# Two buffers for a state space's scratch tile and rotation tables, and another PSUM bank for its last products

## The chip, the cores and the metric

The kernel runs on one core of one Trainium2 chip. The metric is device time in microseconds (us) of one execution: the median of several runs. The core has a matrix engine (TensorE, PE in the profile, with PEld for its weight loads), a vector engine (VectorE, DVE), a scalar engine (ScalarE, ACT), GpSimd (POOL) and a queue engine (SyncE, SP) that issues most of the transfers. Each runs its own instructions in a fixed order, and they wait for one another by semaphores.

## What is computed

One inference step of one hybrid decoder layer (width 1024) for a new prompt of 512 positions and for eight running sequences that get one token each. Cut to what matters here:

```python
def hybrid_layer(x, c, ssm_s0, attend, lp):
    mod = jnp.dot(jax.nn.silu(c), lp['w_ada']) + lp['b_ada']
    sh1, sc1, gt1, sh2, sc2, gt2 = jnp.split(mod, 6, axis=-1)
    proj = jnp.dot(modulate(x, lp['norm_attn'], sh1, sc1), lp['w_in'])
    u, q, k_c, v_c, k_s, v_s, k_w, v_w, g = jnp.split(proj, offsets, axis=-1)
    o_ssm, s_last = ssm_mixer(u, ssm_s0, lp)             # complex diagonal state space, 32 groups
    o_attn, win_state = attend(q, gates, kv_cmp, kv_slc, kv_win)   # sparse attention
    mix = jnp.concatenate([rmsnorm(o_ssm, ...), rmsnorm(o_attn, ...)], axis=-1)
    x = x + gt1[:, None, :] * jnp.dot(mix, lp['w_out'])
    h2 = modulate(x, lp['norm_mlp'], sh2, sc2)
    x = x + gt2 * jnp.dot(jnp.square(jax.nn.relu(jnp.dot(h2, lp['w_up']))), lp['w_down'])

def ssm_mixer(u, s0, lp):                # per group: s_t = lam * s_(t-1) + B u_t ;  y_t = Re(C s_t) + d u_t
    ...
    z = jax.nn.gelu(y)
    return z * jax.nn.sigmoid(jnp.dot(z, lp['ssm_w_glu'])), s_last
```

## The kernel before, in words

Activations lie transposed in SBUF, features on the 128 partitions and the 520 positions (512 and 8) along the free side. Large products take every operand as a high and a low part (`split`: ACT casts the high part, DVE subtracts for the low part, L63 and L64) and issue three matmuls for each pair of tiles. PSUM has eight banks. In the first part of the kernel they are shared out by tag: `pj` 2, `ss` 2, `tr` 2, `ad` 1, `po` 1; `pst(tag, name)` takes the next bank of a tag and so waits until its last user has been read.

The stages follow each other roughly like this: preparation and the projection of `u` (L605 with tile `pj`, to 120 us); the compression of cached keys and values (`compressed`, L382 to L402: transposes `pxc` L368, evictions `xc` on ACT and DVE, products `ph` L387, then `pk` L396 and L398 in the bank `po`); the state space, which runs among it; the projections of keys and values (`kv_proj(0..2)`, loads `wkv` L627, products `pkv` L647) and of the conditioning (`ada`, loads `wada` L330, products `pada` L334); the projection of q (`proj_half`, L605 again, evictions `ql` and `QS` L912 to L914); attention of the prompt (scores `pst` L1217 to L1219, maxima `mxa` L1223, exponentials `pe` L1227, scaling L1232, transposes `ptp` L1246, evictions `PT` L1249, products `po` L1253) woven with that of the eight sequences (`pkT` L1023, `ktS` L1026 and L1028, `pS` L1032, `tS` L1034 and L1010, `smx` L1009, `ppt` L1049, `ptS` L1050, `ppn` L1052); the output projection (`pwo`); and from 525 us the MLP (`pup`, `pdn`, L1401).

Ahead of the state space the values `u` are written to DRAM through the scratch tile `ut` (tag `tmp`, L616) and read back regrouped as `U` (L722 to L725). The state space itself takes the 32 groups in eight **quads** of four groups. A quad makes, on DVE, the tables `BP` and `Cb` through `tmp` (L752 to L759); on PE the products `pm` and transposes `pbb` (L766, L767), evicted as `M0` and `Bb`; from `M0`, through DRAM, the Toeplitz matrix `Tz` (L772, L774); the rotation tables `CT` and `ST` (L776 to L781, from `cmul`, L486 to L488); then `pvs` = Bb x U (L792), evicted as `Vs`, turned by CT and ST into `W`, scanned along time (`Rr`, L803), turned back into `Sx` (L808 to L815); and last the products `pys` (L819: U with Tz, L820: Sx with Cb, eight matmuls in turn), evicted as `ys` (L821) and written to DRAM (L822). After the last quad the final states go through `psf` (L827) and the tile `so` (L828) out to DRAM. `state_space_outputs` (L884 and on) reads the results back one quarter at a time as `yc` (L888), one buffer, and makes `yf` (L890, L893) and the GELU `zt` (L108 to L113); one quarter follows each of `kv_proj(1)`, `kv_proj(2)` and the two halves of the projection of q.

In SBUF most tiles of the state space have one buffer each; `ss`, with two banks, serves `pm0`, `pbb`, `pvs`, `pys` and `psf` of the state space and, later, parts of attention (`psc`, `pS`, `poS`).

The order of instructions on each engine is not that of the code. The program is laid out by a scheduler that simulates a timeline: an instruction is placed when its operands and its buffer are free by the simulated times. So a buffer more or less can change what stands where on all five engines.

Of the kernel before, what the change touches and what calls it, by code (L numbers as in the profile page):

```python
# [9 lines left out]
F32 = mybir.dt.float32  # L10
# [6 lines left out]
P = 128  # L17
D = 1024
T = 512
# [17 lines left out]
def body(tc, i, o, dbg=None):  # L37
# [19 lines left out]
    def pst(tag, name):  # L57
        return bank["tile"].tile([P, 512], F32, tag=tag, name=name, bufs=bank["tags"][tag])
# [9 lines left out]
    def rawt(name):  # L68
        return raw.tile([P, 2048], F32, tag="raw", name=name)
# [101 lines left out]
    def wsplit(r, more=0):  # L171

        if more:
            h, l = (bank["wq"].tile([P, KT, P], F32R, tag="wq" + c, name="wq" + c, bufs=2) for c in "HL")
        else:
            h, l = whl(*r.shape[1:])
        split(h, l, r)
        return h, l
# [34 lines left out]
    GQ = 4  # L213
# [222 lines left out]
    ss = p0.tile([P, 5], F32, name="ss")  # L436
# [48 lines left out]
    def cmul(outr, outi, ar_, ai_, br_, bi_, tmp):  # L485
        nc.vector.tensor_tensor(outr, ar_, br_, ALU.mult)  # L486
        nc.vector.tensor_tensor(tmp, ai_, bi_, ALU.mult)
        nc.vector.tensor_tensor(outr, outr, tmp, ALU.subtract)  # L488
        nc.vector.tensor_tensor(outi, ar_, bi_, ALU.mult)
        nc.vector.tensor_tensor(tmp, ai_, br_, ALU.mult)  # L490
        nc.vector.tensor_tensor(outi, outi, tmp, ALU.add)
# [102 lines left out]
    sl = slx.enter_context(tc.tile_pool(name="sl", bufs=1, reuse_waits="tile"))  # L594
# [3 lines left out]
    def proj_half(wh, wl):  # L598

        for hf in range(2):  # L600
            ps = pst("pj", "pj")
            hc = slice(hf * HB, (hf + 1) * HB)
            for k in range(KT):
                for n, (w, x) in enumerate(((wh, hH), (wh, hL), (wl, hH))):
                    nc.tensor.matmul(ps[:, 0:HB], w[:, k], x[:, k, hc], start=(k == 0 and n == 0), stop=(k == KT - 1 and n == 2))  # L605
            yield hf, ps[:, 0:HB]

    for s in range(2):
        r = rawt("wu").rearrange("p (k c) -> p k c", k=KT)
        nc.sync.dma_start(r, i["w_in"][0, :, s * 256 : (s + 1) * 256].rearrange("(k p) c -> p k c", p=P))  # L610
        for m in range(2):
            wh, wl = wsplit(r[:, :, m * P : (m + 1) * P])
            q = 2 * s + m
            for hf, ps in proj_half(wh, wl):
                nc.scalar.copy(uT[:, q, hf * HB : (hf + 1) * HB], ps)
            ut = sl.tile([P, T], F32, tag="tmp", name="ut")  # L616
            nc.vector.tensor_copy(ut.rearrange("p (t c) -> p c t", t=8), uT[:, q, 0:T].rearrange("p (c t) -> p c t", t=8))
            nc.sync.dma_start(uscr[q * P : (q + 1) * P, 0:T], ut)
            nc.sync.dma_start(uscr[q * P : (q + 1) * P, T:NT], uT[:, q, T:NT])
# [107 lines left out]
    for qd in range(NG // GQ):  # L727
# [14 lines left out]
        b4 = [P, GQ, 8, 16]  # L742
# [4 lines left out]
        def vec_b(x):  # L747
            return x.unsqueeze(2).to_broadcast(b4)

        tmp = sl.tile(b4, F32, tag="tmp", name="tmp")  # L750
        BP = sl.tile(b4, F32, tag="BP", name="BP")
        nc.vector.tensor_tensor(BP, lam_b(lr, 0), vec_b(P1[:, gs]), ALU.mult)  # L752
        nc.vector.tensor_tensor(tmp, lam_b(li, 0), vec_b(P1p[:, gs]), ALU.mult)
        nc.vector.tensor_tensor(BP, BP, tmp, ALU.subtract)
        tmp = sl.tile(b4, F32, tag="tmp", name="tmp")
        Cb = sl.tile(b4, F32, tag="Cb", name="Cb")
        nc.vector.tensor_tensor(Cb, lam_b(lr, 1), vec_b(C1[:, gs]), ALU.mult)
        nc.vector.tensor_tensor(tmp, lam_b(li, 1), vec_b(C1p[:, gs]), ALU.mult)
# [14 lines left out]
        mw = mscr[qd, 0:P]  # L773
        nc.sync.dma_start(Tz, bass.AP(tensor=mw.tensor, offset=mw.offset, ap=[[GQ * 16, P], [16 * GQ * 16, 8], [1, GQ * 16]]))  # L774

        CT = sl.tile([P, GQ, 8, 8], F32, tag="CT", name="CT")  # L776
        ST = sl.tile([P, GQ, 8, 8], F32, tag="ST", name="ST")
        tq = sl.tile([P, GQ, 8, 8], F32, tag="tq", name="tq")
        b8 = [P, GQ, 8, 8]
        ab = [tab[:, x, 1, gs].unsqueeze(3).to_broadcast(b8) for x in range(2)] + [tab[:, x, 0, gs].unsqueeze(2).to_broadcast(b8) for x in range(2)]  # L780
        cmul(CT, ST, *ab, tq)  # L781
        CT = CT.rearrange("p g a b -> p g (a b)")
        ST = ST.rearrange("p g a b -> p g (a b)")
        rho = sl.tile([P, GQ, 64], F32, tag="rho", name="rho")
# [13 lines left out]
        W2 = sl.tile([P, GQ, 64], F32, tag="W2", name="W2")  # L798
        nc.vector.tensor_tensor(W, Vs[:, :, 0:64], CT, ALU.mult)
        nc.vector.tensor_tensor(W2, Vp, ST, ALU.mult)  # L800
        nc.vector.tensor_tensor(W, W, W2, ALU.add)
# [6 lines left out]
        nc.gpsimd.memset(Sx[:, :, 0:1], 0.0)  # L808
        nc.vector.tensor_tensor(W2, Rp, ST, ALU.mult)
        nc.vector.tensor_tensor(W, Rr, CT, ALU.mult)  # L810
        nc.vector.tensor_tensor(Sx[:, :, 1:65], W, W2, ALU.subtract)
# [1 line left out]
        nc.gpsimd.memset(Sx[:, :, 64:72], 0.0)  # L813
        nc.vector.tensor_copy(Sx[:, :, 72:80], s0[:, :, gs].rearrange("p b g -> p g b"))
        ys = sl.tile([P, GQ, 80], F32, tag="ys", name="ys")  # L815
        py = pst("ss", "pys")
        for g in range(GQ):
            c = slice(g * 80, (g + 1) * 80)
            nc.tensor.matmul(py[:, c], Tz[:, :, :, g].rearrange("p t c -> p (t c)"), U[:, qd * GQ + g], start=True, stop=False)  # L819
# [5 lines left out]
    for n in range(2):  # L825
        nc.tensor.transpose(px[:, n * P : (n + 1) * P], sn[:, 4 * n : 4 * n + 4].rearrange("p b g -> p (b g)"), ident)
    nc.tensor.transpose(px[0:NG, 256:384], SF, ident)  # L827
    so = sl.tile([P, 384], F32, name="so")  # L828
    nc.vector.tensor_copy(so[:, 0:256], px[:, 0:256])
    nc.vector.tensor_copy(so[0:NG, 256:384], px[0:NG, 256:384])  # L830
    for n, nm in enumerate(("re", "im")):
# [485 lines left out]
    for n in range(16):  # L1317
        j, br, hh = n // 4, n // 2 % 2, n % 2
        if n % 4 == 0:
            po = pst("po", "po")  # L1320
# [275 lines left out]
```

## Time and profile before

| | |
|---|---|
| median of 3 runs | 896.05 us (895.32 to 898.2) |
| the profiled execution | 896.29 us, its span 894.6 us |
| granted clock over the span (share of full) | 0.992 |
| PE busy | 844.3 us, 94% |
| DVE busy | 525.0 us, 59% |
| ACT busy | 388.2 us, 43% |
| POOL busy | 65.2 us, 7% |
| state space: first `pvs`, last `pys` | 138.5 us, 258.4 us |
| projection of q, attention, output projection, MLP begin | 267, 297, 451, 525 us |

The span is the profiled part of the execution; the time of the execution is 1.69 us longer. An engine is busy while at least one of its instructions is executing, so a stretch minus PE's busy time in it is the time in which PE did nothing.

### The profile page before, as it was taken

The numbers are of one execution on the slowest core, as the hardware profiler recorded it, in microseconds if no ns is written. First come the engines' busy times: TensorE is split into PE (matmuls) and PEld (weight loads), VectorE is DVE, ScalarE is ACT, GpSimd is POOL, SyncE is SP. The second block draws the span as 40 slices with busy tenths as digits, with TensorE's granted clock in tenths as the row PEclk, the third lists the DMA queues.
The fourth block names the chain that finished last, engine by engine and source line by source line (L and its number), as shares of the span: only waits on it lengthen the run. The fifth ranks groups of instructions, "written<-read, shape, count | busy, mean of one in ns | idle before, by whom it ended". The sixth has DMA issues, their size and how long they took to land.

```text
span 894.6 us, 16415 instructions
## 1 busy us (share of the span) xinstructions
PE 844.3 (94%) x6517; PEld 747.3 (84%) x6517; DVE 525.0 (59%) x1413; ACT 388.2 (43%) x880; POOL 65.2 (7%) x147
## 2 busy tenths in 40 slices
PE   3799998999999899999889999999999999999995
PEld 2567897788998676756579999999999999999995
DVE  6676656759747975667578964443233444434534
ACT  2545326634435656546655554441111344433422
POOL 6001201000134200100000000000000000000000
PEclk9999999999999999999999999999999999999998
DMA  8956678366456620303257552333333333332202
GB/s 294 318 193 217 194 169 239 123 204 194 127 179 206 203 95 1 142 1 142 78 206 227 161 189 85 95 95 95 95 95 95 95 95 95 96 88 70 79 1 95
DMA packets 111836, 122.36 MB, mean 137 GB/s; under 512 B 24500, under 2 KB 91880, under 8 KB 109584
## 3 DMA queue, kind: packets, MB, share of 16 engines
q1 hardware_dynamic: 102256, 89.71, 33.0%
q0 software_dynamic: 5488, 29.99, 9.8%
q10 hardware_dynamic: 4016, 1.62, 0.7%
q8 instruction: 51, 0.84, 0.4%
q14 instruction: 25, 0.20, 0.1%
HBM read 112.47 MB, written 13.03 MB: 140 GB/s over the span
## 4 chain that ended last, share of the span: by engine, by line
PE 86%; DMA 6%; ACT 3%; DVE 2%; issue 1%; SPq 0%; ACTq 0%; DVEq 0%
PE pdn L1401 21%; PE pup L1401 20%; PE pj L605 5%; PE pwo L1401 5%; PE pkv L647 5%; PE ph L387 5%; DMA wada<-w_ada 5%; PE pada L334 2%; PE ptp L1246 2%; PE po L1253 2%; PE pS L1032 2%; PE pg L1273 2%; PE pst L1217 2%; PE pys L819 2%; PE pkT L1023 1%; PE pst L1218 1%
## 5 line engine op out<-in xcount | busy, mean ns | idle before, releaser
L1401 PE MATMUL pdn<-hidL,wH 128*128 128x256 f32 (+1 forms) x480 | 136.1, 284 | 0.0
L1401 PE MATMUL pdn<-hidH,wL 128*128 128x256 f32 (+1 forms) x480 | 135.9, 283 | 0.0
L1401 PE MATMUL pdn<-hidH,wH 128*128 128x256 f32 (+1 forms) x480 | 135.4, 282 | 0.0
L1401 PE MATMUL pup<-h2L,wH 128*128 128x256 f32 (+1 forms) x480 | 135.0, 282 | 0.0
L1401 PE MATMUL pup<-h2H,wL 128*128 128x256 f32 (+1 forms) x480 | 135.0, 282 | 0.0
L1401 PE MATMUL pup<-h2H,wH 128*128 128x256 f32 (+1 forms) x480 | 134.1, 283 | 0.0
L1401 PEld LDWEIGHTS pup<-h2L,wH 128*128 128x128 f32 x480 | 90.4, 188 | 0.8 <-DVE rs_t L97 0.8
L1401 PEld LDWEIGHTS pdn<-hidH,wL 128*128 128x128 f32 x480 | 90.6, 189 | 0.0
L1401 PEld LDWEIGHTS pdn<-hidL,wH 128*128 128x128 f32 x480 | 90.4, 188 | 0.1
L1401 PEld LDWEIGHTS pup<-h2H,wL 128*128 128x128 f32 x480 | 90.4, 188 | 0.0
L1401 PEld LDWEIGHTS pdn<-hidH,wH 128*128 128x128 f32 x480 | 90.4, 188 | 0.0
L1401 PEld LDWEIGHTS pup<-h2H,wH 128*128 128x128 f32 x480 | 89.6, 188 | 0.0
L63 ACT CAST wH<-wdn 128x1024 fp32r<-128x1024 f32 x30 | 31.5, 1050 | 114.0 <-PE pdn L1401 104.1
L64 DVE TENSOR_TENSOR wL<-wup,wH 128x1024 fp32r<-128x1024 f32 x30 | 36.7, 1224 | 58.1 <-ACT wH L63 58.1
L64 DVE TENSOR_TENSOR wL<-wdn,wH 128x1024 fp32r<-128x1024 f32 x30 | 36.8, 1225 | 54.2 <-ACT wH L63 54.2
L387 PE MATMUL ph<-xc,w 128*128 128x256 f32 (+2 forms) x320 | 65.4, 356 | 1.2 <-DVE xc L377 0.7
L387 PEld LDWEIGHTS ph<-xc,w 128*128 128x128 f32 x320 | 52.8, 203 | 12.9 <-issue 6.4
L63 ACT CAST wH<-wup 128x1024 fp32r<-128x1024 f32 x30 | 31.5, 1050 | 48.0 <-PE pup L1401 37.6
L1479 ACT ACTIVATE rl<-pup 128x256 f32<-128x256 f32 (+1 forms) x64 | 24.4, 384 | 48.9 <-PE pup L1401 48.8
L375 ACT COPY xc<-pxc 64x256 f32<-64x256 f32 x96 | 32.1, 366 | 20.8 <-DVE xc L377 18.2
L1410 DVE SCALAR_TENSOR_TENSOR xT<-pdn,mod,xT 128x256 f32<-128x256 f32 x32 | 15.2, 479 | 43.2 <-PE pdn L1401 43.2
L1480 DVE TENSOR_TENSOR rl<-rl 128x256 f32<-128x256 f32 (+1 forms) x64 | 27.1, 425 | 22.6 <-ACT rl L1479 22.6
(557 smaller groups left out, 2023.9 us busy)
## 6 DMA issues: line engine op xcount, KB each, us to landing
wada<-w_ada SPq DMA_DIRECT2D x20, 1024.0 KB
wup<-w_up SPq DMA_DIRECT2D x16, 1024.0 KB
wdn<-w_down SPq DMA_DIRECT2D x16, 1024.0 KB
wo<-w_out SPq DMA_DIRECT2D x8, 1024.0 KB
wada<-w_ada SPq DMA_DIRECT2D x8, 512.0 KB
rwin<-state_win SPq DMA_DIRECT2D x4, 1024.0 KB
new_win_sample<-state_win POOLq DMA_DIRECT2D x2, 2044.0 KB, 8.9
wkv<-w_in SPq DMA_DIRECT2D x3, 1024.0 KB
```

What stands on the lines that cost most here:

```text
L63: nc.scalar.copy(h, src)
L64: nc.vector.tensor_tensor(l, src, h, ALU.subtract)
L334: nc.tensor.matmul(ps[k % 4 * 32 : k % 4 * 32 + 32], cT[:, k], rs[k // kp][:, k % kp], start=(k < 4), stop=(k >= 4))
L375: nc.scalar.copy(dst[:, :, :, hf], srcv[:, :, :, hf])
L387: nc.tensor.matmul(phv[:, lo:hi, 0:w], w1[n][:, r_], xc[n][:, lo:hi, r_ % 8, off : off + w], start=(r_ == 0), stop=(r_ == 15))
L605: nc.tensor.matmul(ps[:, 0:HB], w[:, k], x[:, k, hc], start=(k == 0 and n == 0), stop=(k == KT - 1 and n == 2))
L647: nc.tensor.matmul(ps[0:mp, 0:nw], x[:, k, tok], w[:, k % 4], start=(k == 0 and n == 0), stop=(k == KT - 1 and n == 2))
L819: nc.tensor.matmul(py[:, c], Tz[:, :, :, g].rearrange("p t c -> p (t c)"), U[:, qd * GQ + g], start=True, stop=False)
L1032: nc.tensor.matmul(S[b4 * 32 : b4 * 32 + 32], q4[:, 4 * grp + b4], kts[b4], start=True, stop=True)
L1401: nc.tensor.matmul(ps[:, 0 : b - a], w, x[:, a:b], start=first and n == 0, stop=last and n == 2)
L1479: nc.scalar.activation(rl, ps[:, 0 : b - a], AF.Relu)
L1480: nc.vector.tensor_tensor(rl, rl, rl, ALU.mult)
```

## The change

```diff
-            ut = sl.tile([P, T], F32, tag="tmp", name="ut")
+            ut = sl.tile([P, T], F32, tag="tmp", name="ut", bufs=2)
...
-        tmp = sl.tile(b4, F32, tag="tmp", name="tmp")
+        tmp = sl.tile(b4, F32, tag="tmp", name="tmp", bufs=2)
         BP = sl.tile(b4, F32, tag="BP", name="BP")
...
-        tmp = sl.tile(b4, F32, tag="tmp", name="tmp")
+        tmp = sl.tile(b4, F32, tag="tmp", name="tmp", bufs=2)
         Cb = sl.tile(b4, F32, tag="Cb", name="Cb")
...
-        CT = sl.tile([P, GQ, 8, 8], F32, tag="CT", name="CT")
-        ST = sl.tile([P, GQ, 8, 8], F32, tag="ST", name="ST")
+        CT = sl.tile([P, GQ, 8, 8], F32, tag="CT", name="CT", bufs=2)
+        ST = sl.tile([P, GQ, 8, 8], F32, tag="ST", name="ST", bufs=2)
...
-        py = pst("ss", "pys")
+        py = pst("po", "pys")
...
-    so = sl.tile([P, 384], F32, name="so")
+    so = sl.tile([P, 384], F32, tag="tmp", name="so", bufs=2)
```

The scratch tile of the `u` writes and of the tables (`ut`, `tmp`) gets two buffers, and `so` becomes one more user of them; `CT` and `ST` get two buffers each; `pys` moves from the two banks `ss` to the one bank `po`, which the products `pk`, `pkp` and `pvp` of the compression use in the same stretch and the attention's products later. The instructions are the same ones, and as many; no loop changes. What changes is the order in which the scheduler lays them out, from early in the state space up to the output projection. From the start of the MLP's first pass the order of PE is that of before.

Three places show it. The first is PE at the start of the state space: `pvs` (L792) and `pys` (L819, L820) of the quads, with `pm` and `pbb` (L766, L767) of the next quads and the compression's `pxc` and `ph` between. Before:

```order
L792 MATMUL pvs<-U,Bb 128x72 x4
L368 MATMUL pxc<-ident,rc 128x128 x8
L334 MATMUL pada<-wada,cT 32x512 x4
L368 MATMUL pxc<-ident,rc 128x128 x4
L819 MATMUL pys<-U,Tz 128x80
L766 MATMUL pm_1644<-C_136,BP 128x16 x4
L368 MATMUL pxc<-ident,rc 128x128 x4
L339 MATMUL padt<-ident,mrow 128x128 x4
L767 MATMUL pbb<-ident,BP 128x128 x4
L387 MATMUL ph<-xc,w_155 128x2x128 x4
L368 MATMUL pxc<-ident,rc 128x128 x4
L387 MATMUL ph<-xc,w_155 128x2x128 x5
```

And now:

```order
L792 MATMUL pvs<-U,Bb 128x72 x4
L766 MATMUL pm_1644<-C_136,BP 128x16 x4
L368 MATMUL pxc<-ident,rc 128x128 x4
L819 MATMUL pys<-U,Tz 128x80
L368 MATMUL pxc<-ident,rc 128x128 x4
L767 MATMUL pbb<-ident,BP 128x128 x4
L368 MATMUL pxc<-ident,rc 128x128 x4
L334 MATMUL pada<-wada,cT 32x512 x4
L368 MATMUL pxc<-ident,rc 128x128 x4
L792 MATMUL pvs<-U,Bb 128x72 x4
L766 MATMUL pm_1786<-C_136,BP 128x16 x4
L368 MATMUL pxc<-ident,rc 128x128 x4
```

The second quad's `pvs` now stands ahead of the rest of the first quad's `pys`; before it stood behind all of them, after the last row shown. `pada` has moved from one place behind the first `pvs` to several.

The second place is DVE where attention starts: `yf` (L890, L893) and the GELU steps `zt` (L109, L110) are those of the last quarter of the state space's results, `mxa` (L1223) is the first maximum of attention's scores. Before:

```order
L914 TENSOR_TENSOR QS<-ql,QS 64x252
L986 COPY q_3372<-qs 64x8x4
L914 TENSOR_TENSOR QS<-ql,QS 64x252
L1223 TENSOR_REDUCE mxa<-pst 128x1
L999 TENSOR_TENSOR gsel_3385<-pgs,hm 64x24
L890 SCALAR_TENSOR_TENSOR yf<-uT,vec,yc 128x512
L893 SCALAR_TENSOR_TENSOR yf<-uT,vec,yc 128x8
```

And now:

```order
L914 TENSOR_TENSOR QS<-ql,QS 64x260
L890 SCALAR_TENSOR_TENSOR yf<-uT,vec,yc 128x512
L893 SCALAR_TENSOR_TENSOR yf<-uT,vec,yc 128x8
L914 TENSOR_TENSOR QS<-ql,QS 64x260
L109 TENSOR_SCALAR zt<-zt 128x520
L982 MEMSET q_3372 128x256
L110 TENSOR_TENSOR zt<-zt,yf 128x520
L991 COPY knT<-pkn 128x16
L1109 MEMSET pen_4095 128x16
L1109 MEMSET pen_4106 128x16
L986 COPY q_3372<-qs 64x8x4
L1223 TENSOR_REDUCE mxa<-pst 128x1
```

The last `yf` and half of its GELU now stand ahead of the first maximum instead of behind it.

The third place is DVE near the end of attention: `smx` (L1009) is the maximum of the last scores of the eight sequences, on which `tS` (L1010, ACT) and `ppt` (L1049, PE) hang; `wL` (L64) splits a piece of the output weights. Before:

```order
L1034 TENSOR_TENSOR tS<-pS,pen_4106 128x512
L1232 TENSOR_SCALAR pe<-pe,dn 128x128
L1232 TENSOR_SCALAR pe<-pe,dn 128x256
L1232 TENSOR_SCALAR pe<-pe,dn 128x384
L1232 TENSOR_SCALAR pe_4959<-pe_4959,dn 128x512
L1223 TENSOR_REDUCE mxa<-pst 128x1
L1009 TENSOR_REDUCE smx<-tS 128x1
L1223 TENSOR_REDUCE mxa<-pst 128x1 x3
L64 TENSOR_TENSOR wL<-wo,wH 128x1024
```

And now:

```order
L1232 TENSOR_SCALAR pe_4959<-pe_4959,dn 128x512
L1223 TENSOR_REDUCE mxa<-pst 128x1
L1042 TENSOR_TENSOR tS<-psn,nmask 128x8
L1223 TENSOR_REDUCE mxa<-pst 128x1 x2
L1034 TENSOR_TENSOR tS<-pS,pen_4106 128x512
L64 TENSOR_TENSOR wL<-wo,wH 128x1024
L1009 TENSOR_REDUCE smx<-tS 128x1
L1223 TENSOR_REDUCE mxa<-pst 128x1
```

The last L1034, which reads the last `pS`, comes behind the scalings instead of ahead of them, and the weight split has moved from behind `smx` to ahead of it.

## Rows read from the trace of the kernel before

**Rows 1.** The page's sections 1 and 4: busy time by engine, the chain.

```profile
PE 844.3 (94%) x6517; PEld 747.3 (84%) x6517; DVE 525.0 (59%) x1413; ACT 388.2 (43%) x880; POOL 65.2 (7%) x147
PE 86%; DMA 6%; ACT 3%; DVE 2%; issue 1%; SPq 0%; ACTq 0%; DVEq 0%
```

**Rows 2.** Busy time of each engine by stretch (start:end, length, engines, clock, DMA).

```profile
core 0: us, PE busy (x) PEld busy (x) DVE busy (x) ACT busy (x) POOL busy (x), PEclk, DMA share, GB/s
...
133.30:145.80 12.50, 9.97 (x84) 7.48 (x82) 8.99 (x28) 10.76 (x32) 2.86 (x4) 1.00 1.04 243
145.80:167.00 21.20, 21.20 (x117) 19.33 (x116) 12.65 (x36) 7.45 (x20) 1.02 (x6) 1.00 0.35 116
167.00:185.00 18.00, 16.82 (x117) 13.26 (x116) 11.79 (x30) 14.01 (x41) 0.99 (x4) 1.00 0.80 256
185.00:221.00 36.00, 36.00 (x259) 29.50 (x259) 29.24 (x78) 12.81 (x29) 2.16 (x10) 1.00 0.55 174
221.00:267.00 46.00, 46.00 (x360) 44.02 (x360) 29.98 (x85) 18.81 (x55) 11.70 (x28) 1.00 0.53 153
267.00:297.00 30.00, 28.60 (x207) 24.25 (x206) 23.40 (x48) 17.48 (x44) 13.77 (x30) 1.00 0.64 194
297.00:320.00 23.00, 19.75 (x120) 13.36 (x122) 19.50 (x70) 13.39 (x40) 2.18 (x9) 1.00 0.48 168
...
400.00:451.00 51.00, 44.87 (x399) 29.79 (x398) 36.03 (x100) 35.70 (x97) 2.84 (x3) 0.99 0.35 124
...
525.00:885.00 360.00, 358.73 (x2999) 358.30 (x2997) 155.52 (x306) 120.83 (x222) 0.00 (x0) 1.00 0.28 83
```

**Rows 3.** PE's waits, 133.3 to 297 us (engine, line, releaser: total us, times, longest).

```profile
PE pvs L792 <- DMA new_cmp_sample<-kvs: 1.5, 1, 1.5
PE pj L605 <- ACT QS L913: 1.4, 1, 1.4
PE pada L334 <- DMA wada<-w_ada: 1.1, 1, 1.1
```

**Rows 4.** Waits of ACT and of DVE for `pys`, 133 to 260 us.

```profile
ACT ys L821 <- PE pys L820: 21.9, 8, 5.0
DVE Cb L757 <- PE pys L820: 15.2, 5, 5.3
```

**Rows 5.** The tile `tmp`: what its engine sat idle for before it.

```profile
  DMA uscr<-ut: 1.2, 1
```

**Rows 6.** Timeline of SP, ACT, PE: the second `wkv` load to its use.

```profile
205.22 0.52 SPq L627 DMA_DIRECT2D wkv<-w_in  x1
...
212.60 1.99 ACT L63 CAST wH<-wkv 128x1024 fp32r<-128x1024 f32 x2 [2.40 <-DMA wkv<-w_in]
...
220.88 0.38 PE L647 MATMUL pkv<-wH,hH 128*128 128x256 f32 x1
```

**Rows 7.** Timeline of ACT ahead of PE's wait for `QS`.

```profile
278.12 0.64 ACT L111 ACTIVATE zt<-zt 128x520 f32<-128x520 f32 x1 [2.03 <-DVE zt L110]
```

**Rows 8.** Start of attention: PE's waits, 297 to 320 us, then DVE's timeline.

```profile
PE pst L1217 <- ACT pe L1227: 1.9, 3, 1.1
PE pkT L1023 <- ACT ktS L1028: 0.7, 1, 0.7
...
298.02 1.08 DVE L890 SCALAR_TENSOR_TENSOR yf<-uT,vec,yc 128x512 f32<-128x512 f32 x1
...
304.21 0.67 DVE L110 TENSOR_TENSOR zt<-zt,yf 128x520 f32<-128x520 f32 x1
```

**Rows 9.** End of attention: PE's waits, 400 to 451 us, then DVE's timeline.

```profile
PE po L1253 <- ACT PT L1249: 3.7, 4, 1.9
PE ppt L1049 <- ACT tS L1010: 1.4, 2, 1.1
PE ppn L1052 <- ACT ptS L1050: 0.8, 1, 0.8
...
435.71 1.21 DVE L64 TENSOR_TENSOR wL<-wo,wH 128x1024 fp32r<-128x1024 f32 x1
```

## The prediction

> **What bounds the kernel now.** I read the page's busy times and chain first, then a table of busy time by stretch, then PE's waits stretch by stretch, and last the waits of the engines beside it. PE is busy 94% of the span and holds 86% of the chain that ended last [rows 1]. So an edit that removes no PE work can gain only where PE sits idle. The table by stretch says where that is [rows 2]: length minus PE busy is 2.53 us in 133.3 to 145.8, nothing in 145.8 to 167, 1.18 in 167 to 185, nothing in 185 to 267, 1.40 in 267 to 297 (the projection of q), 3.25 at the start of attention (297 to 320), 6.13 at its end (400 to 451), and 1.27 in the MLP's 360. The state space, where the edit is made, runs from 138 to 258 us, and PE idles there about 3.7 us in all. The waits that the diff points at are large and lie elsewhere: ACT sits 21.9 us for `pys` before its eight `ys` evictions, DVE 15.2 us for `pys` before it may overwrite `Cb` [rows 4]. Both are waits *for* PE, by engines with room, while PE does the compression and the projections. Shortening them doesn't shorten PE's work.
>
> **The change part by part.** No instruction is added or removed, so the sum is made only of idle time that goes or comes. It is made against the profiled execution, 896.29 us, of which 894.6 are the span; the median of the runs shown lies 0.24 below it.
>
> *Second buffer of `tmp` and `ut`.* DVE waited for this tile once, 1.2 us, until the last write of `u` had left it [rows 5]. The wait goes; PE's first `pvs` doesn't come earlier, because it waits for a transfer (1.5 us, put down by the profile to a small DMA [rows 3]; by place it is the landing of `U`), which hangs on that same write and not on `tmp`. Directly: 0.
>
> *Second buffers of `CT` and `ST`, `pys` in a bank of its own.* These let the next quad be prepared while the last one's `pys` still waits. No wait for a free `CT` or `ST` stands among the costly ones, and the wait for `Cb` remains, since `Cb` keeps its one buffer. What follows is the new order, so I go through it by stretch.
>
> *133 to 146.* The `pada` products that waited 1.1 us for their weights directly behind the first `pvs` [rows 3] now stand several rows later, so that wait is covered: up to -1.1. Four of the `pxc` that stood before the first `pvs` are now behind it, and its wait for `U` grows by what they took, some 0.5 (9.97 us for 84 matmul records are 0.12 each [rows 2]). ACT is busy 10.76 of the 12.5 us here [rows 2] and evicts `pxc`, so PE may come to wait for ACT instead. Between -1.1 and +0.6; I take **-0.3**.
>
> *146 to 267.* PE has nothing to gain in 145.8 to 167 and after 185, and 1.18 between, where ACT is busy 14.01 of 18 us with the same evictions [rows 2]. Bounds -1.2 and +0.5; I take **0**. What does happen: the chain of the eight quads has less to wait for, and I expect the last `pys` some 10 us earlier than 258.4 (in the new order it stands ahead of the products of `kv_proj(2)`, not among them). PE fills the place with projection work that it has to do anyway.
>
> *The second `wkv` load.* On SP it stands behind the `Tz` read of the sixth quad in the new order, directly with the third load, instead of ahead of it. Before, it was issued at 205.2, ACT waited 2.40 us for it to begin its cast at 212.6, and PE used it from 220.9 [rows 6]: 8.3 us of slack behind the cast's start, most of which the new order takes away. Cast and subtraction of the first half need about 2.3 of it (the cast is half of 1.99, the subtraction 1.2 as for the output weights [rows 9]). If the load comes as late as its use allows, PE waits. From 0 to +2; I take **+0.3**.
>
> *Projection of q.* PE's one wait is 1.4 us for the eviction `QS` [rows 3]. ACT was late because it had sat 2.03 us for DVE's `zt` step [rows 7], with a weight cast and other evictions still to do. DVE was late with that step because `yf` waited for `yc`, and `yc` for the last quads. With these 10 us earlier the 2.03 goes. Against it, the new order of ACT puts a GELU step, a `KH` cast and the weight cast between two pairs of evictions where there was the weight cast alone. From -1.4 to 0; I take **-0.7**.
>
> *Start of attention, 297 to 320.* DVE is busy 19.5 of 23 us, PE waits 1.9 us for exponentials and 0.7 for `ktS`, which hang on DVE's maxima and on ACT [rows 2, 8]. The order puts the last `yf` (1.08 us) and one long GELU step (0.67) [rows 8] ahead of the first maximum: 1.75 us of DVE leave the stretch. At most these 1.75 reach PE; at least none does, if what ends last is ACT's exponentials in their own order. I take **-1.0**. The cover for the moved steps is the projection of q, where DVE has 6.6 us free of 30 [rows 2].
>
> *End of attention and output projection.* The scheduler has drawn the order anew here too. PE waits 1.4 us for `tS` before `ppt`, 0.8 for `ptS` and 3.7 for `PT` [rows 9]. The last `pS` now stands close ahead of `ppt`, and DVE has the weight split (1.21 us [rows 9]) between reading it and `smx`: that wait can grow by 1.2 or so. ACT in turn has two exponentials ahead of `tS` that stood behind it, so less is left after. From -1 to +2; I take **+0.5**. The MLP stays as it is.
>
> Sum: -0.3 + 0 + 0.3 - 0.7 - 1.0 + 0.5 = -1.2. From 896.29 that is 895.1, and against the median, 0.24 less: **894.8 us**.
>
> [...]
>
> **The rivals.**
> *PE's full stretches are not full (faster).* PE's busy time counts overlapping matmuls, and their ends are modelled. In 185 to 221 PE shows 36.00 of 36.00 us, its weight loads 29.50; in the MLP's 360 us both are above 358 [rows 2]. If half of these 6.5 us between are hidden gaps that an earlier chain closes, the gain grows by 3.3: 891.5. For it: the state space runs in that stretch. Against: no wait of PE there is among its listed ones [rows 3], and loads that are shorter than their matmuls leave the same picture. The same time comes out if the two start-of-attention and projection waits go whole (-1.75 and -1.4) with the front's -1.1, and the end loses nothing: -4.25, 891.8. [...]
>
> *The end of attention pays (slower).* The new place of `smx` delays `tS`; `ppt` then waits 1.2 us more, `ptS` and `ppn` 0.8 once more, and one `PT` eviction that ACT reaches late costs its 1.9 again [rows 9]: +3.9, and with only the -0.3 of the front to set against it +3.6: 899.7. It decides when the last `pS` ends less than about 2.4 us of PE work ahead of `ppt` (the split's 1.21 [rows 9], and a maximum over 1032 columns, which I estimate at the same from the split's 1024). For it: the new order has some fourteen PE rows between, with few long ones. Against: two exponentials now precede `tS`, which frees ACT behind it.
>
> *Nothing moves (no change).* The chain ends earlier, yet PE's waits at the attention start are ACT's and stay; small gains and losses cancel: 896.
>
> That the edit doesn't do what it says: with `pk` and `pys` in one bank a quad can wait for the compression's eviction. In the new order each `pk` stands between two quads, never inside one, so this costs nothing I can see.
>
> **How the numbers follow.** Forecast, small gain at 894.8 (892.8 to 896.5): 0.40. No change at 896: 0.14. More gain, about 891.5: 0.29. Slower, about 899.7: 0.17. About 0.3%, or 2.7 us, is what a measurement of this kernel can tell from none. Below 893.4 lie most of the third case and a little of the first: 0.33. Above 898.7 most of the last: 0.15. Between: 0.52. The range, 890.5 to 899.2, leaves out about 0.08 below and 0.10 above.
>
> **What would show it.** In the new profile: last `pys` near 248 us; DVE's wait for `Cb` and ACT's for `pys` smaller; PE idle in the state space still 2.5 to 4 us; `yf` of the last quarter ahead of the first `mxa`, and PE's wait for `pe` at the start of attention under 1 us; the wait at `pj` gone or halved; the wait at `ppt` above 1.1. It would be wrong if PE's first MLP product starts over 3 us earlier or later than now, or if PE shows a new wait in 185 to 267.

## The result, and the profile after

The changed kernel takes 905.42 us (median of 4 runs, 902.88 to 906.81), the kernel before 895.68 beside it: a ratio of 1.0092, interval 1.0069 to 1.0116. It is slower by 0.9%, where 894.8 us and a small gain were forecast. Its profiled execution takes 906.81 us, with a span of 905.1, 10.5 us more than the 894.6 of before. The page's first section of the changed kernel answers to [rows 1]:

```profile
PE 849.3 (94%) x6517; PEld 750.4 (83%) x6517; DVE 526.0 (58%) x1413; ACT 388.9 (43%) x880; POOL 66.2 (7%) x147
```

The instructions are as many as before, but PE is busy for 849.3 us instead of 844.3, and the span less the busy time, its idle time, is 55.8 instead of 50.3. So the 10.5 us are 5.5 of idle time and 5.0 of the same work done more slowly. To see where, both traces are cut at the same events: the first `pvs`, the first `pst` of attention, the first `pwo` of the output projection, the first `pup` of the MLP, the end of the MLP. In each line the length less PE's busy time is its idle time, and PEclk the granted clock. First the kernel before:

```profile
0.00:138.51 138.51, 113.99 (x797) 91.09 (x797) 90.17 (x307) 57.00 (x124) 23.86 (x50) 0.99 0.76 228
138.51:296.38 157.87, 154.22 (x1099) 134.76 (x1099) 111.57 (x286) 76.67 (x205) 32.11 (x79) 1.00 0.58 178
296.38:449.81 153.43, 143.39 (x1039) 94.29 (x1037) 102.87 (x319) 92.97 (x254) 9.27 (x18) 1.00 0.28 101
449.81:503.47 53.66, 52.08 (x414) 50.78 (x413) 44.80 (x129) 28.63 (x52) 0.00 (x0) 0.97 0.61 197
503.47:883.73 380.26, 379.83 (x3170) 375.63 (x3168) 171.82 (x359) 130.59 (x244) 0.00 (x0) 1.00 0.31 93
```

and the changed kernel at the same events:

```profile
0.00:137.10 137.10, 110.43 (x789) 88.30 (x789) 93.48 (x314) 55.24 (x118) 24.73 (x50) 1.00 0.77 232
137.10:298.39 161.29, 158.32 (x1108) 137.17 (x1108) 108.45 (x276) 77.43 (x208) 31.71 (x81) 0.99 0.56 174
298.39:455.47 157.08, 145.98 (x1038) 96.41 (x1037) 103.43 (x322) 93.90 (x256) 9.77 (x17) 0.98 0.27 98
455.47:509.83 54.36, 50.84 (x414) 49.62 (x412) 46.06 (x132) 30.00 (x55) 0.00 (x0) 1.00 0.62 204
509.83:894.25 384.42, 383.00 (x3168) 378.15 (x3168) 170.85 (x356) 129.97 (x243) 0.00 (x0) 0.99 0.30 91
```

The stretch from the first `pvs` to attention is 3.4 us longer, attention 3.7, the output projection 0.7, the MLP 4.2 (the first stretch is 1.4 shorter, of which 1 us is eight `pxc` that now stand behind the first `pvs`). The MLP's matmuls are those of before, and still it takes 4.2 us more. Its first product starts at 503.47 us in the kernel before, not at 525 as the table of times before has it. Nor is the order of PE the old one from there on: the first 238 matmuls of the MLP stand in another order too, and only behind them (from 533 us before, 542 now) is it the same. What stands ahead of it are PE's waits. The longest of those that are new or longer than before, from its waits in 133 to 320 us and in 398 to 515 us (total, times, longest):

```profile
PE pvs L792 <- DMA Tz<-mscr: 2.5, 1, 2.5
...
PE ppt L1049 <- ACT tS L1010: 2.4, 1, 2.4
PE pup L1401 <- ACT h2H L200: 2.1, 1, 2.1
...
PE pup L1401 <- DVE h2L L201: 0.7, 1, 0.7
```

Each of these three places is followed by a stretch at half clock (PEclk 0.50), which begins 1.5, 1.3 and 0.9 us behind the end of the wait of 2.5, 2.4 and 2.1 us. The three long waits and the four half-clock stretches of the changed kernel up to the end of the MLP, as lines of the table by stretch (the one at 316 us follows waits of PE for `pe`):

```profile
134.62:137.10 2.48, 0.01 (x2) 0.03 (x1) 0.00 (x0) 1.27 (x4) 0.00 (x0) 1.00 1.22 221
138.63:142.04 3.41, 3.41 (x18) 3.41 (x18) 2.27 (x6) 2.51 (x8) 0.39 (x1) 0.50 0.35 121
316.12:319.54 3.42, 3.42 (x10) 2.63 (x9) 3.00 (x15) 1.03 (x5) 0.00 (x0) 0.50 0.00 0
438.80:441.17 2.37, 0.00 (x1) 0.01 (x1) 1.39 (x3) 1.30 (x3) 0.00 (x0) 1.00 0.01 3
442.42:445.83 3.41, 3.33 (x41) 2.29 (x45) 1.06 (x4) 0.52 (x2) 0.00 (x0) 0.50 0.02 5
507.73:509.83 2.10, 0.00 (x1) 0.00 (x0) 2.10 (x7) 1.08 (x3) 0.00 (x0) 1.00 0.47 180
510.68:517.51 6.83, 6.22 (x34) 5.55 (x38) 5.88 (x19) 3.10 (x7) 0.00 (x0) 0.50 0.49 156
```

That is 17.07 us at half clock. The kernel before has two such stretches of 3.41 us between its start and the end of the MLP, one at 40 us, far ahead of the change, and one behind a wait of 1.94 us for `PT`:

```profile
446.66:448.60 1.94, 0.01 (x1) 0.01 (x2) 1.94 (x2) 1.94 (x4) 0.00 (x0) 1.00 1.09 370
449.68:453.09 3.41, 3.41 (x14) 2.84 (x13) 3.41 (x12) 2.32 (x7) 0.00 (x0) 0.50 1.03 381
```

In the trace of tmp_alone, a run described below, matmuls of one kind follow each other nearly twice as slowly at half clock (213 ns from start to start instead of 112; the rows are in the last section). From that I estimate that about half of such a stretch is lost: (17.07 - 6.82) / 2 = 5.1 us more than before. With the 5.5 us of idle time that makes 10.6 us, where 10.5 were measured. By this estimate the new waits cost twice, by their length and by the clock behind them.

### The profile page after: what moved, and what is told of

It reads as the page before. It is cut to its first block, busy times and chain, and to the rows that moved or that the text cites. A ratio compares the mean times of both kernels' runs of the same rounds, so it can differ in the third digit from the quotient of the medians.

```text
span 905.1 us, 16413 instructions
## 1 busy us (share of the span) xinstructions
PE 849.3 (94%) x6517; PEld 750.4 (83%) x6517; DVE 526.0 (58%) x1413; ACT 388.9 (43%) x880; POOL 66.2 (7%) x147
## 4 chain that ended last, share of the span: by engine, by line
PE 62%; DVE 5%; DMA 2%; ACT 2%; issue 1%; SPq 0%; DVEq 0%; ACTq 0%
PE pup L1401 20%; PE pdn L1401 20%; PE pwo L1401 5%; PE po L1253 2%; PE ptp L1246 2%; PE pS L1032 2%; PE pg L1273 2%; DMA yc<-yscr 1%; PE pkT L1023 1%; PE pst L1217 1%; DMA new_win_prompt<-kvt 1%; PE pst L1218 1%; PE poS L1121 1%; DVE yf L890 0%; DVE mxa L1223 0%
## 5 line engine op out<-in xcount | busy, mean ns | idle before, releaser
L1401 PE MATMUL pup<-h2H,wH 128*128 128x256 f32 (+1 forms) x480 | 136.2, 285 | 2.3 <-ACT h2H L200 2.1
L64 DVE TENSOR_TENSOR wL<-wup,wH 128x1024 fp32r<-128x1024 f32 x30 | 36.7, 1225 | 62.7 <-ACT wH L63 62.7
L64 DVE TENSOR_TENSOR wL<-wdn,wH 128x1024 fp32r<-128x1024 f32 x30 | 36.8, 1225 | 54.2 <-ACT wH L63 54.2
L387 PE MATMUL ph<-xc,w 128*128 128x256 f32 (+2 forms) x320 | 63.2, 347 | 0.7 <-DVE xc L377 0.7
L1227 ACT ACTIVATE pe<-pst,mxa 128x512 f32<-128x512 f32 (+1 forms) x64 | 33.5, 530 | 16.9 <-DVE mxa L1223 11.8
L1410 DVE SCALAR_TENSOR_TENSOR xT<-pdn,mod,xT 128x256 f32<-128x256 f32 x32 | 15.2, 479 | 43.2 <-PE pdn L1401 43.2
```

What stands on the lines that cost most here:

```text
L64: nc.vector.tensor_tensor(l, src, h, ALU.subtract)
L387: nc.tensor.matmul(phv[:, lo:hi, 0:w], w1[n][:, r_], xc[n][:, lo:hi, r_ % 8, off : off + w], start=(r_ == 0), stop=(r_ == 15))
L1227: nc.scalar.activation(at(qt, 0, nk), d, AF.Exp, bias=mx[:, qt : qt + 1], accum_out=dn[:, qt : qt + 1])
L1401: nc.tensor.matmul(ps[:, 0 : b - a], w, x[:, a:b], start=first and n == 0, stop=last and n == 2)
L1410: nc.vector.scalar_tensor_tensor(xT[:, m, a:b], ps[:, 0 : b - a], mod[:, g0 + m, 0:1], xT[:, m, a:b], ALU.mult, ALU.add)
```

## The experiments

Two devices are used in most of them. The first holds the program in a given order: behind the traced program each engine's instructions are tied to a list, one behind the other, by edges that set the order of issue and add no wait of their own. So an order can be moved from one kernel to another, whole or for the instructions of some stages. The second fills a gap of PE with useless transposes of some 0.12 us (eight `pxc` of that shape take 1.04 us in the kernel before, from 139.43 us on) into the PSUM tile whose real products come next and overwrite them.

```diff
-        body(tc, i, o)
+        body(tc, i, o); replay(tc)          # the order, as a list of instructions by engine
...
         pvv = pst("ss", "pvs")
+        if qd == 0: fill(nc, pvv[:, 0:P], ident, 24)     # only in the runs that fill a gap
```

Theory one: the buffers and the bank cost nothing; the new order of issue does, at a few places. Rivals: the buffers themselves, the state space's new order as a whole, any new order at all. In the table the ratio is to the kernel before, run beside it on the same chip.

| run | what is in it | median us | ratio (interval) |
|---|---|---|---|
| the change | everything | 905.42 | 1.0092 (1.0069 to 1.0116) |
| buffers_old_order | buffers of the change without the bank, order of before | 896.28 | 0.9995 (0.9968 to 1.0021) |
| after_entry_old | new order, old from the output projection on | 901.07 | 1.0036 (1.0017 to 1.0055) |
| after_attention_old | new order, old from attention on | 900.79 | 1.0045 (1.0019 to 1.0071) |
| before_attention_new | old order, new from attention on | 902.08 | 1.0058 (1.0037 to 1.0078) |
| before_entry_new | old order, new from the output projection on | 900.44 | 1.0046 (1.0022 to 1.0070) |
| tmp_alone | `tmp`, `ut`, `so` with two buffers | 915.19 | 1.0208 (1.0148 to 1.0268) |
| ct_st_alone | `CT`, `ST` with two buffers | 916.78 | 1.0211 (1.0166 to 1.0256) |
| pys_bank_alone | `pys` in the bank `po` | 898.36 | 1.0019 (0.9989 to 1.0050) |
| after_gaps_filled | the change, three gaps filled | 902.53 | 1.0064 (1.0030 to 1.0097) |
| front_gap_filled | after_attention_old, first gap filled | 898.67 | 0.9999 (0.9976 to 1.0022) |
| before_gap_filled | the kernel before, first gap filled | 896.43 | 0.9976 (0.9953 to 0.9998) |
| after_both_mended | after_entry_old, first gap filled | 900.73 | 1.0034 (1.0021 to 1.0047) |
| pys_bank_entry_old | pys_bank_alone, old from the output projection on | 894.53 | 0.9980 (0.9959 to 1.0001) |
| pys_bank_both_mended | the same, first gap filled | 895.89 | 0.9980 (0.9969 to 0.9991) |

**The buffers without the order.** 

> tmp, CT, ST and so as changed (two buffers each), pys left in the banks ss; every engine's instructions are held in the order of the kernel before. Theory (the order costs the 9.4 us, the buffers nothing): as before, about 896 us within 2. Rival (the buffers themselves cost, by where they lie in SBUF or whom they share it with): 899 us or more.

Measured 0.9995: as before, within 0.3%. In the old order the second buffers cost nothing and bring nothing that these runs can tell. (The bank `po` can't be tried in the old order: there a `pk` of the compression stands inside a quad's `pys`, in the same bank. It was tried in an order of its own, below.)

**The order by stages.** 

> The changed kernel in its own order, but what belongs to the output projection and the step into the MLP stands in the order of the kernel before (the two broadcast products bc again 26 matmuls ahead of the MLP's first product, not directly ahead of it). Theory: PE's idle time of 2.10 and 0.72 us at that step goes, and with it the 6.83 us at half clock behind it, which cost some 3.4: 905.4 - 6.2 = about 899 us. Rival (the step is only where a loss from further ahead comes to light): 904 us or more.

> The kernel before with its buffers and its order, but what belongs to the output projection and the step into the MLP stands in the changed kernel's order (bc directly ahead of the first pup, the reciprocal root's steps on DVE with weight splits between them). The mirror of the run that put this step back. Theory (this step costs 5 us whatever stands ahead of it: 2.82 us of idle PE, and a half-clock stretch behind it in most executions, 1.7 us for each 3.41): 901 us where the kernel before has 896.8. Rival (it costs only behind the changed front): 898.5 us or less.

Measured 1.0036 and 1.0046. The step into the MLP, put back, takes (1.0092 - 1.0036) = 0.56%, 5.0 us, from the changed kernel (6.2 were expected), and put into the kernel before it costs 0.46%, 4.1 us: so it costs 4 to 5 us whatever stands ahead of it. The order has changed on two engines there. PE's `bc` (L1372) spreads the reciprocal root `rs` over the partitions, from the tile `dg` that ACT makes of the root; DVE's `hf` hangs on `bc`, and the first `h2H` on `hf`. The changed kernel's DVE in front of `bc`:

```profile
500.84 0.16 DVE L99 SCALAR_TENSOR_TENSOR rs_y<-rs_t,rs_y 128x2 f32<-128x2 f32 x1
501.00 1.23 DVE L64 TENSOR_TENSOR wL<-wup,wH 128x1024 fp32r<-128x1024 f32 x1
502.14 0.15 DVE L97 SCALAR_TENSOR_TENSOR rs_t<-rs_y 128x2 f32<-128x2 f32 x1
...
503.02 1.22 DVE L64 TENSOR_TENSOR wL<-wup,wH 128x1024 fp32r<-128x1024 f32 x1
504.15 0.15 DVE L98 TENSOR_TENSOR rs_t<-rs_t,rs_x 128x2 f32<-128x2 f32 x1
...
504.34 0.16 DVE L99 SCALAR_TENSOR_TENSOR rs<-rs_t,rs_y 128x2 f32<-128x2 f32 x1
```

Two weight splits of 1.2 us stand between the last steps of the root. In the kernel before, the last step comes at 496.79, with the first of these splits behind it at 496.89. On PE `bc` stands behind all of the output projection, with nothing left to do while `h2H` is made:

```profile
504.81 0.68 ACT L1371 ACTIVATE dg<-ident,rs 128x128 f32<-128x128 f32 x2
...
507.00 0.29 PE L1401 MATMUL pwo<-mixH,wqL 128*128 128x264 f32 x1
507.13 0.61 PE L1372 MATMUL bc<-dg,ones 128*128 128x128 f32 x4
...
508.77 0.86 DVE L199 SCALAR_TENSOR_TENSOR hf<-xT,A,bc 128x256 f32<-128x256 f32 x2
...
509.83 0.50 PE L1401 MATMUL pup<-h2H,wH 128*128 128x256 f32 x2 [2.10 <-ACT h2H L200]
```

where the kernel before has 26 more `pwo` matmuls to run. In this trace it is the place of `bc` on PE that decides, and not DVE's splits: `dg` was done at 505.49 us, 1.6 us before PE came to `bc`. Behind `bc` DVE adds 1.0 us, from the end of `bc` at 507.74 to `hf` at 508.77; in the kernel before `hf` follows at once (500.58 and 500.62). Both engines were put back together, so their shares were not measured apart.

> The changed kernel with its own order up to the projection of q; attention, output projection and the step into the MLP in the order of the kernel before. Theory: all but the front's part of the loss goes, which is one stretch of 3.41 us at half clock, 1.7 us: about 897.5 us. Rival (the new state space is to blame, by PE or by what it leaves late): 901 us or more.

> The mirror of that: buffers and order of the kernel before up to the projection of q, then attention, output projection and the step into the MLP in the changed kernel's order. Nothing of the change is in it but the order behind the state space. Theory: 905.4 - 1.7 = about 903.5 us. Rival (the state space is to blame): 898 us or less.

Measured 1.0045 and 1.0058, 3 us more and 1.5 less than the theory. So the state space's order costs about 4 us, not the 1.7 of one half-clock stretch: the theory had it too small. In its profile there are 10.24 us at half clock behind the first `pvs` and at the start of attention, where the kernel before has none, and over the whole span no more idle time:

```profile
137.67:144.50 6.83, 6.83 (x36) 5.52 (x35) 4.20 (x11) 5.03 (x15) 1.23 (x2) 0.50 0.30 107
301.51:304.92 3.41, 3.29 (x8) 1.32 (x8) 1.93 (x8) 0.28 (x1) 0.00 (x0) 0.50 0.80 307
```

**The clock.** 

> The changed kernel in its own order, with useless products in three of PE's gaps: 18 transposes of 0.12 us before the first pvs (gap 2.48 us), 18 before the last ppt (2.37 us), 22 before the first pup (2.10 and 0.72 us). They write into the tile that the real products behind them overwrite. Nothing is taken away, PE does some 7 us more work. Theory (the clock falls to half after such gaps, and that is where half the loss is): no half-clock stretch behind these three places, where the changed kernel had 3.41, 3.41 and 6.83 us; about 5 us faster than the changed kernel in that execution and 3 to 5 in the median: 901 to 903 us. Rival (the gaps cost only their own length, the clock falls for other reasons): as the changed kernel, 905 us, or slower.

Measured 1.0064: 2.9 us less than the change in the medians, with intervals that overlap. In its profile no half-clock stretch stands behind the three filled places. The lines from the first `pvs`, the last `ppt` and the first `pup` on show the clock:

```profile
138.07:144.00 5.93, 5.85 (x47) 4.62 (x48) 4.20 (x10) 4.52 (x13) 1.68 (x2) 1.00 0.49 170
441.00:446.00 5.00, 4.76 (x90) 3.40 (x88) 1.85 (x8) 1.82 (x6) 0.00 (x0) 1.00 0.00 0
507.00:515.00 8.00, 7.32 (x69) 7.10 (x71) 7.60 (x19) 4.73 (x9) 0.00 (x0) 1.00 0.59 202
```

But two stretches, 3.41 and 6.83 us, came elsewhere in attention, the second of them reaching into the output projection, so this run alone settles little. The next two are cleaner.

> As the run with the changed kernel's order up to the projection of q and the old order behind it (900.8 us, 0.45% above the kernel before), and 24 useless transposes of 0.12 us, 2.9 us in all, in the gap of 2.47 us before the first pvs. Theory (the front's loss is the clock: without half-clock time and idle time its stretch takes as long as the old front's): no half-clock stretch within 8 us behind the first pvs, where there were 6.83 us; 898 to 899 us. Rival (the front's new order costs in PE's busy time itself): 900.8 us or more, with the first pst no earlier.

> Control: the kernel before in its own order, with 16 such transposes, 1.9 us, in its gap of 1.46 us before the first pvs. Theory: nothing to gain, since in most executions no half-clock stretch stands behind that gap; 896 to 897.5 us. Rival (the filling itself buys time, by making the load of U or the clock better in general): 894.5 us or less.

Measured 0.9999 and 0.9976. The filling takes 0.46% from the kernel with the new front, but 0.24% from the kernel before too. So the control missed: its 896.43 us lie in the forecast, but the kernel before beside it was at 898.13, and there was something to gain. The old front has half clock behind this gap in some executions: none in the trace of the kernel before, 3.41 us in that of before_entry_new, which has the same front.

With both gaps filled the new front is still 2.2 us slower in the medians (898.67 against 896.43, run beside each other; 1.5 in the means, and the single runs overlap). Their traces are each the fastest of 12 executions: with the new front there is no half-clock stretch up to the end of the MLP, with the old one none from 44 us on. The 2 us can be seen in traces that have no half clock from their start to the first `pst`. With the old front (before_attention_new, buffers_old_order):

```profile
0.00:294.81 294.81, 265.04 (x1896) 223.74 (x1896) 202.24 (x593) 133.59 (x328) 55.33 (x129) 1.00 0.66 203
...
0.00:294.90 294.90, 265.78 (x1896) 224.19 (x1896) 202.18 (x593) 133.68 (x328) 56.66 (x129) 1.00 0.67 203
```

and with the new one and its gap filled (front_gap_filled, after_both_mended, a run that follows below):

```profile
0.00:297.16 297.16, 270.45 (x1919) 227.57 (x1919) 204.81 (x592) 133.05 (x327) 57.35 (x131) 1.00 0.66 201
...
0.00:298.10 298.10, 270.52 (x1919) 226.91 (x1919) 203.77 (x594) 133.67 (x329) 56.50 (x128) 1.00 0.66 200
```

Less the 2.9 us of filling PE is busy for 267.6 us with the new front, and for 265.0 and 265.8 with the old one, for the same matmuls. So of the front's 4 us about half goes with the gap and the clock behind it. Some 2 us stay, and in these traces they lie in PE's busy time, as the rival has it; why the same matmuls take longer in the new order is not shown.

**Each part alone.** 

> Only tmp, ut and so with two buffers; the scheduler draws its own order. In it the tables of the first quad come ahead as in the changed kernel, so fewer products stand before the first pvs, and at the step into the MLP the two bc products stand 26 matmuls ahead of the first pup, as before. Theory (the step into the MLP costs 5 us, the front 3 to 4): PE's gap before the first pvs near 2.4 us, none of 2.1 before the first pup, time about 900 us where the kernel before has 897. Rival (any new order costs about the same): 904 us or more.

> Only CT and ST with two buffers. The order up to the first two quads is that of before; at the step into the MLP the bc products stand directly ahead of the first pup, as in the changed kernel. Theory: gap before the first pvs near 1.5 us, gap of about 2 us before the first pup, 5 us lost there: about 902 us. Rival (the loss comes with the front's order alone): 898 us or less.

> Only pys moved to the bank po. The second quad's pvs comes early as in the changed kernel, with the order ahead of the first pvs as before; bc directly ahead of the first pup. Theory: as with CT and ST alone, about 902 us; more only if pys in the bank po costs by itself, which the traces give no sign of. Rival (the shared bank is the cause): 905 us or more, with PE or the compression's pk waiting for ys.

Measured 1.0208, 1.0211 and 1.0019. The first two are wrong by 15 us, the third by 4 the other way. The gaps named did appear (2.77 and 1.98 us before the first `pvs`; 2.10 before the first `pup` with CT and ST, none with `tmp`), but the order of attention that these two edits drew is far worse than any other. The stretch from the first `pst` to the first `pwo`, for `tmp` alone and for CT and ST alone:

```profile
305.64:471.94 166.30, 150.46 (x1037) 100.67 (x1035) 107.71 (x330) 94.92 (x257) 12.05 (x20) 0.93 0.32 110
...
294.92:465.61 170.69, 152.39 (x1036) 99.70 (x1035) 107.30 (x330) 94.51 (x257) 11.93 (x20) 0.93 0.31 107
```

Against 153.43 us before, 13 and 17 us more: the idle time is 15.8 and 18.3 instead of 10.0, and 23.9 us of each are at half clock. With `tmp` alone another 9 us lie ahead of attention, where 27.3 us are at half clock. No part of the change touches an instruction of attention. And the parts do not add up: 18, 20 and 2 us alone, 8 to 10 together. The bank `po` shows no cost of its own: the move alone is at 1.0019, within its interval of nothing, and no wait of PE or of `pk` for `ys` shows. But it was only run with an order of its own, which loses at the step into the MLP and gains in attention.

**What is left, and a better version.** 

> pys in the bank po and nothing else of the change, in the order that the scheduler drew for that edit alone, with the output projection and the step into the MLP put back into the order of the kernel before. That edit alone lost 2.82 us at the step and a half-clock stretch behind it, and gained 4 us in attention. Theory: 898.4 - 4.5 = about 894 us, 3 us faster than the kernel before. Rival (the step's order is paid for elsewhere, or attention's gain was the draw of one execution): 897 us or more.

> The changed kernel's order in the state space and in attention; output projection and step into the MLP in the old order; 24 useless transposes of 0.12 us in the gap before the first pvs. Theory (the two places are the whole loss): within 0.2% of the kernel before, 896 to 898.5 us where that is 897. Rival (the new order of attention costs by itself, 1.3 us of idle PE before ppt and a half-clock stretch more in it): 899.5 us or more.

> pys in the bank po and nothing else of the change, output projection and step into the MLP in the old order, 16 useless transposes before the first pvs. Without the filling this was at 0.998 of the kernel before, and filling the kernel before gave 0.9976. Theory (both add up): 0.9955, about 893.5 us where the kernel before is at 897.5. Rival (both are the same few microseconds of half-clock time, which can be taken away once): 0.9975, 895.3 us.

Measured 0.9980, 1.0034 and 0.9980. With the step into the MLP and the front's gap mended the changed kernel is still 3 us slower than before, so the two places are not the whole loss. The front's rest of some 2 us, above, is in it. Whether attention's new order costs too, as the rival has it, three pairs of runs say, each differing in that order alone. after_both_mended against front_gap_filled gives +0.35%, before_attention_new against before_entry_new +0.12%, and after_entry_old against after_attention_old, run beside each other, -0.09%. In the first pair the stretch of attention is 154.89 instead of 153.48 us long, its idle time 10.71 instead of 10.12, and 6.83 us of half clock come behind its waits for `tS` (2.36 us) and `PT` (2.19 us); but front_gap_filled waits 2.01 us for `PT` too, with no half clock behind it. From nothing to 3 us is what can be said of attention. The mended version with the `pys` bank is 0.2% faster than the kernel before (interval 0.9969 to 0.9991), and so is the kernel before with its first gap filled (0.9953 to 0.9998); the two gains do not add up, as the rival had it.

## Why the prediction was wrong

Two steps failed. That "the sum is made only of idle time that goes or comes" priced a wait at its length and took PE's work to run at one speed: 10.2 us more at half clock cost 5 us of PE's busy time. And "The MLP stays as it is" put the step into the MLP at nothing: it cost 4 to 5 us.

**What bounds the kernel**: right. PE's instructions are fixed, buffers shorten waits of ACT and DVE for PE, and the direct effect is nothing that can be measured (buffers_old_order). The last `pys` came at 248.4 us as forecast, ACT's wait for `pys` fell from 21.9 to 16.9 us and DVE's from 15.2 to 10.3 [rows 4], and none of it reached the end.

**133 to 146 us**: the idle time went as worked out, the clock did not. The wait for `wada` went, the wait at the first `pvs` grew by 1.0 instead of 0.5 (eight `pxc` moved behind it, not four). The term said -0.3; the front cost about +4 us, some 2 of them by the wait and the clock behind it and some 2 in PE's busy time. Here, as everywhere in the sum, idle time was priced at its length alone. The trace of before had the price in it, in the stretch at 449.7 us, and its PEclk row was not read for it.

**146 to 267**: 0 was forecast, and a new wait came, for `kvt` at 264.66 us (the tile's eviction on ACT had waited 2.96 us for its last write to DRAM). PE's waits in the changed kernel from 133 to 320 us:

```profile
PE pst L1217 <- ACT pe L1227: 1.7, 2, 1.4
PE pkt L682 <- ACT kvt L675: 1.3, 1, 1.3
```

That was one of the prediction's own signs of being wrong. The other was a first MLP product over 3 us away from its old time; it came 6.4 us later.

**The second `wkv` load**: no wait of PE for it; 0 instead of +0.3.

**Projection of q**: -1.4 instead of -0.7. PE's 1.4 us wait for `QS` [rows 3] is gone; the new one for `kvt` takes nearly as much.

**Start of attention**: -1.0 was forecast, next to nothing came. The last `yf` does stand ahead of the first maximum, but it starts at 296.73 us instead of 298.02 [rows 8]. The quads' results were ready 10 us sooner; reading them back was not. DVE's waits in the changed kernel from 262 to 300 us:

```profile
DVE yf L890 <- DMA yc<-yscr: 4.6, 2, 2.5
```

4.6 us instead of 2.3: with one buffer for `yc` each quarter's read waits for the last `yf`, and takes 7 and 4.5 us of the chain. PE waited 1.7 us for `pe` (1.9 before [rows 8]), and a half-clock stretch followed at 316.

**End of attention**: the mechanism of the rival, at its place, and for its first term with its size. The wait before `ppt` was to grow by 1.2 us and grew from 1.06 to 2.37. The rest of that rival's 3.9 us did not come (`PT` 3.0 instead of 3.7, `ppn` 0.2 instead of 0.8), and half-clock time came in its stead.

**Output projection and MLP**: the largest miss. "The MLP stays as it is" holds for its instructions, not for its start nor for the order of its first 238 matmuls: the `bc` had moved by 26 places on PE just ahead of it, and the new order showed that before any run. With 2.82 us of idle time and 6.83 us at half clock behind it this is 6.2 of the 10.5 us in the profiled execution, 4 to 5 in the medians. (Two short waits at 543 and 544 us, 0.7 together, are new as well; one of 0.4 is gone.) It stands in no term of the sum and in no rival.

**The rivals**: that PE's full stretches hide gaps, and that an earlier chain closes them, is not borne out. PE's busy time less half of the half-clock time is 844.3 - 3.4 = 840.9 us before and 849.3 - 8.5 = 840.8 after. So close an agreement is in part luck: the same sum, the filling taken off, lies between 837 and 843 in most other runs. The rival of a slower time named one of four places and no clock; its 899.7 and the range's end of 899.2 were both too low.

## What to carry to other kernels

Where a scheduler sets the order, a buffer more is a new draw of the order of everything behind it, and its effect can lie hundreds of microseconds from the edit: compare the orders at every hand-over between stages, above all where a short chain on another engine stands between two full stretches of PE. An idle gap of about 2 us on PE mostly cost more than its length in this kernel: of 31 gaps of 1.9 us or more in these 16 traces, between 120 us and the end of the MLP, 22 had a half-clock stretch at their end or within 2 us behind it (in the kernel before and the changed one 4 of 5). If half of a stretch is lost, as estimated above, one of 3.41 us costs 1.7 us and one of 6.83 costs 3.4. So look in the trace of before whether a half-clock stretch stands behind gaps of the size that a change may bring, and price a new gap by what is seen there. To judge the edit itself, run it in the old order.

## What the runs showed of the hardware

The same wait is not always followed by half clock. The gaps of 2.10 and 0.72 us before the first `pup` had 6.83 us of half clock behind them in the changed kernel, 3.41 in before_entry_new, and none in before_attention_new. PE's wait for `PT` near the end of attention, 1.9 to 2.5 us in 14 traces, had one in 6 of them. What made the difference is not shown. Runs of one program differ by several microseconds with it: of the twelve of before_entry_new the two longest, 906.6 and 906.8 us, have a granted clock of 0.983 over the span, the others, 898.2 to 903.6, 0.989 to 0.992. A gap of 1.38 us before the first `pvs` had half clock 2.2 us behind it in pys_bank_entry_old, and one of 1.46 had none in the kernel before.

Half clock came without a gap too. In the trace of tmp_alone, where no wait of PE shows from 205 to 235 us, PE ran 17.07 us at half clock without a moment of idle time, while it did 42 of the prompt's compression products `php` (128x62), `pada` (128x512) and products of the state space (128x80 and narrower). The stretch, then `php` in a row at full clock just ahead of it and at half clock within it:

```profile
213.36:230.43 17.07, 17.07 (x79) 15.01 (x79) 9.65 (x26) 3.77 (x7) 0.47 (x3) 0.50 0.31 97
...
209.98 2.00 PE L697 MATMUL php<-xTp,w 128*128 128x62 f32 x16
...
214.70 3.94 PE L697 MATMUL php<-xTp,w 128*128 128x62 f32 x18
```

The 16 start 112 ns apart, the 18 start 213 ns apart. Why the clock fell there was not tried.
